# A hybrid attention block: 128-row products for the low part of k, operands at one place in 512 bytes, and a second half of w_out that enters early

## The chip, the cores and the metric

The kernel runs on one core of a Trainium2 chip. The metric is the device time of one execution in microseconds. Three runs of the kernel before gave a median of 910.77 us (908.93 to 912.34). TensorE is called PE, VectorE DVE, ScalarE ACT, GpSimd POOL, and SyncE SP; PEld is PE's loading of weights.

## The reference, cut to what matters

The block has 512 tokens of width 1024, 8 attention heads of 64, 8 retention heads with keys of 64 and values of 128, and an inner width of 4096. All data is fp32.

```python
ada = (c_act @ w_ada[l] + b_ada[l])[:, None, :]
sh1, sc1, g1, sh2, sc2, g2 = jnp.split(ada, N_ADA, axis=-1)
h = modulate(rms_norm(x, ln1_w[l]), sh1, sc1)
proj = h @ w_in[l]
mq, mk, mv, rq, rk, rv, rg, ga, gr = jnp.split(proj, split_at, axis=-1)
mq = apply_rotary(to_heads(mq, MOBA_HEADS), moba_cos, moba_sin)
mk = apply_rotary(to_heads(mk, MOBA_HEADS), moba_cos, moba_sin)
a_out = moba_attention(mq, mk, to_heads(mv, MOBA_HEADS))   # scores q.k, softmax, times v
y_a = from_heads(a_out) @ w_moba_o[l]
rq = apply_rotary(to_heads(rq, RET_HEADS), ret_cos, ret_sin)
rk = apply_rotary(to_heads(rk, RET_HEADS), ret_cos, ret_sin)
r_out = retention_chunkwise(rq, rk, to_heads(rv, RET_HEADS))  # scores q.k, decayed, times v
r_out = head_group_norm(r_out, ret_gn_w[l]).astype(x.dtype)
y_r = (jax.nn.silu(rg) * r_out) @ w_ret_o[l]
merged = jax.nn.sigmoid(ga) * y_a + jax.nn.sigmoid(gr) * y_r
x = x + g1 * (merged @ w_out[l])
h2 = modulate(rms_norm(x, ln2_w[l]), sh2, sc2)
x = x + g2 * (jnp.square(jax.nn.relu(h2 @ w_ff1[l])) @ w_ff2[l])
return rms_norm(x, final_norm_w)
```

## The kernel before

Every fp32 operand of a large product is split in two: a high part, and a low part that holds what the high part leaves. `mm3` (L214) then issues three matmuls, high by high, high by low and low by high, for one 128x512 piece (L215 to L217). A weight comes from HBM by a DMA of SP into one of three `raw` buffers; ACT writes its high part `whi` (L179) and POOL its low part `wlo` in four pieces (L184).

The stages follow each other in the span: the conditioning vector and the first norm (0 to 67 us); attention, with the projections of its heads, up to about 228; retention, with its projections, to 415; the gates to 441.7; the merge of both branches with the first half of w_out's columns, 441.7 to 513.8; w_out's second half with the second norm, to 548; the first product of the MLP (FF1) to 723, the second (FF2) to 897; the last norm.

**Scores.** Two heads are stacked in the 128 partitions. `kh` holds the high part of k for each of the two, with zeros in the other head's 64 partitions, so `q` of both heads meets it in a product of 128 rows (L547, L682). The low part `kl` holds both heads without zeros, and its product takes 64 rows of `kl` and of `q` (L548 and L683). The pieces of work that prepare the next pair of heads wait in a list `later` and are taken one by one between products. A head has four score products, of 128, 256, 384 and 512 columns, each followed by its product with `kl`, so there are 32 products of 64 rows in attention and 32 in retention.

**Merge.** `merge(i2)` (L955) makes 256 columns of y_r (48 matmuls with `zh`, `zl`), and for each of their two halves DVE multiplies by the gate (`sgr`, L958), adds the attention branch (`m`, L960), ACT writes `mh` (L961) and DVE `ml` (L962), the operands of w_out. Between these, `advance(background)` takes one step of `ada_steps`: the gate vector g1 is made by 16 steps of two DVE instructions each (L780, L782, L785), each on a DMA of 256 KB into one of two buffers `ada_raw`; after each four steps comes a split (`ada_hi` on ACT, `ada_lo` on DVE) and two small matmuls on PE (L756, L757). The loop at L968 then follows each of merge 1 to 3 with w_out's first half for the two k that are ready, 12 matmuls for each of eight k, into the four accumulators `wo0`; a scheduler sets the final order in this stage.

**w_out's second half and the second norm.** For each of four row blocks t, `out_product` gives 24 matmuls with `woh` and `wol`, which `load_late` made. After the residual, `square` (ACT) and `scale2` (DVE, L1034 and L1035) norm the block, `turn2` transposes it on PE (L1045) and brings it back by four instructions on DVE (L1052) and four on ACT (L1050), and `split2` writes FF1's operands `h2h` and `h2l` (L223, L224). In this part the order on PE, DVE and ACT is the order of the code.

A tile's address in SBUF follows from the sizes of the tiles that its pool has given out before it.

Of the kernel before, what the change touches and what calls it, by code (L numbers as in the profile page):

```python
# [8 lines left out]
F32 = mybir.dt.float32  # L9
# [18 lines left out]
def block_kernel(  # L28
# [116 lines left out]
    cols = G.tile([P, 72], F32, name="cols")  # L145
    cols1 = G.tile([P, 72], F32, name="cols1")

# [307 lines left out]

    later, stacked = deque(), []

    def do_later(n):
        for _ in range(min(n, len(later))):
            later.popleft()()  # L460

# [25 lines left out]
    def stack_q(i, t):  # L487
# [8 lines left out]
        qk[i] = [q]  # L496

    def stack_k(i, t):
        kh = A1.tile([P, 2, S], F32R, name="kh", tag="kh", bufs=2)
        kl = A1.tile([P, S], F32R, name="kl", tag="kl", bufs=2)  # L500

        def copies(s):
            own, other = halves(s)
            ACT.activation(kh[own, s, :], t[own, :], AF.Copy)
            ACT.activation(kh[other, s, :], t[own, :], AF.Copy)

        def rest(s):
            own, _ = halves(s)
            DVE.tensor_sub(kl[own, :], t[own, :], kh[own, s, :].bitcast(F32))

        later.extend((lambda: copies(0), lambda: rest(0), lambda: copies(1), lambda: rest(1)))
        later.append(lambda: stacked.append(i))
        qk[i] += [kh, kl]

# [22 lines left out]
    def moba_scores(h, t):  # L537

        while h // 2 not in stacked:
            do_later(1)  # L540
        q, kh, kl = qk[h // 2]
        s, pb = h % 2, 64 * (h % 2)
        own = slice(pb, pb + 64)
        n = (t + 1) * P
        ts = slice(t * P, n)
        sc = ps("S")
        PE.matmul(sc[:, :n], q[:, s, ts], kh[:, s, :n], start=True, stop=False)  # L547
        PE.matmul(sc[:, :n], q[own, s, ts], kl[own, :n], start=False, stop=True)  # L548
        pr = A1.tile([P, S], F32, name="pr", tag="pr", bufs=4)
        st = A1.tile([P, 8], F32, name="stat", tag="stat", bufs=6)  # L550
        DVE.tensor_tensor(sc[:, ts], sc[:, ts], cap, op=ALU.min)
# [81 lines left out]

    eh = A1.tile([P, 224], F32R, name="eh")
    es = A1.tile([P, 4], F32R, name="es")
# [35 lines left out]
    def ret_scores(h, kt):  # L671
        while 4 + h // 2 not in stacked:
            do_later(1)
        q, kh, kl = qk[4 + h // 2]
        s, pb = h % 2, 64 * (h % 2)
        own = slice(pb, pb + 64)
        if kt == 0 and h < 7:
# [4 lines left out]
        PE.matmul(sc[:, :n], kh[:, s, js], q[:, s, kt * P :], start=True, stop=False)  # L682
        PE.matmul(sc[:, :n], kl[own, js], q[own, s, kt * P :], start=False, stop=True)  # L683
        pr = A1.tile([P, S], F32, name="pr", tag="pr", bufs=4)
# [55 lines left out]


    mod2 = G.tile([P, 2, 8], F32, name="mod2")

# [211 lines left out]
    def merge(i2):  # L955
        for i, a in enumerate(proj_256(w_ret_o, i2 * 256, NK, zh, zl)):
# [5 lines left out]
            DVE.tensor_sub(ml[k], m32, mh[k].bitcast(F32))  # L962
            advance(background)
            advance(background)

    wo0 = [ps("S"), ps("S"), ps("PT"), ps("O")]
    background = ada_steps(A2, (2,), DVE, g1)
    next(background)  # L968
    merge(0)
    for i2 in range(4):  # L970
# [7 lines left out]
    drain(background)  # L978
    a2_stack.close()
# [24 lines left out]

    def load_late(k):

        raw = load_raw([(lambda t: t[:, 0:512], w_out[k * P : (k + 1) * P, 512:D])])
        hi = H.tile([P, 512], F32R, name=f"woh{k}", tag=f"hh{k}")
        lo = H.tile([P, 512], F32R, name=f"wol{k}", tag=f"hl{k}")
        with tc.issue_after(merged[4 + k // 2]):  # L1010
            split(raw[:, 0:512], hi, lo, ACT, POOL)
        return hi, lo

    for t in range(NT):
        residual(W2, t, 0, wo0[t], g1)
    wo_w = [load_late(k) for k in range(NK)]

    def out_product(t, a, ks):
        ts = slice(t * P, (t + 1) * P)
        for k in ks:  # L1020
            hi, lo = wo_w[k]
            mm3(a, mh[k][:, ts], ml[k][:, ts], hi, lo, k == 0, k == NK - 1)

# [73 lines left out]
    scale2(3)  # L1097
    split2(2, h32)
    first = [ps("acc") for _ in range(4)]
# [166 lines left out]
```

## Time and profile before

| | |
|---|---|
| median of three runs | 910.77 us (908.93 to 912.34) |
| time of the profiled execution | 911.24 us |
| its span | 909.2 us |
| PE busy | 878.2 us, 97% of the span |
| PEld busy | 708.5 us, 78% |
| DVE busy | 465.6 us, 51% |
| ACT busy | 409.1 us, 45% |
| POOL busy | 501.6 us, 55% |
| mean granted clock of PE | 0.994 |

The span runs from the first instruction to the last; the 2.04 us between it and the time of the same execution lie around it. The profiled execution is 0.47 us above the median. Matmuls overlap, so the time that one costs PE is read from start to start, not from its own length. In a row of the timeline the columns are the start in us, the length in us, the engine, the line, the operation, what it writes and what it reads with the shapes, and in brackets the idle time of the engine before it and what ended this. "64*128 64x512" means 64 rows of weights and 64 rows of moving data; a number after x counts instructions that one row stands for.

### The profile page before, as it was taken

Reading aid. Unit: us, or ns where it says so; the run is one execution under the profiler, and the core shown is the slowest. Engines: PE = TensorE matmul, PEld = TensorE weight load, DVE = VectorE, ACT = ScalarE, POOL = GpSimd, SP = SyncE. Lnnn points to the kernel's source line nnn. Section 1 sums busy time; section 2 is a strip of 40 time slices with the busy share of each in tenths; the row PEclk is TensorE's granted clock in tenths of the full one; section 3 lists DMA queues with packets and bytes.
Section 4 is the critical chain, followed back from the end, with each engine's and each line's share of the span. In section 5 each row is a group of like instructions: output and inputs, shape, how many; then the busy total and the mean of one; then the engine's idle time right before and its main releaser. Section 6 shows DMA issues by size and latency. Waiting matters only on the chain.

```text
span 909.2 us, 11772 instructions
## 1 busy us (share of the span) xinstructions
PE 878.2 (97%) x4138; PEld 708.5 (78%) x4138; DVE 465.6 (51%) x887; ACT 409.1 (45%) x697; POOL 501.6 (55%) x606
## 2 busy tenths in 40 slices
PE   7889999999999999999999889999999999999996
PEld 4667777789777888778888679888888888888885
DVE  5885676777776868883186776003304011122225
ACT  4446888986744636645232254222222211112124
POOL 3456343625543654564755475967777754444454
PEclk9899999999999999999999999999999999999999
DMA  9955222321353343422454733533432222222202
GB/s 273 277 152 166 66 77 64 94 70 47 117 160 120 118 149 115 151 71 70 139 172 152 251 109 95 158 98 114 138 102 94 95 93 93 96 95 97 100 30 93
DMA packets 104426, 108.41 MB, mean 119 GB/s; under 512 B 4832, under 2 KB 93232, under 8 KB 104368
## 3 DMA queue, kind: packets, MB, share of 16 engines
q1 hardware_dynamic: 104224, 107.41, 38.2%
q8 instruction: 32, 0.52, 0.2%
q14 instruction: 26, 0.21, 0.1%
q10 hardware_dynamic: 144, 0.26, 0.1%
HBM read 105.55 MB, written 2.10 MB: 118 GB/s over the span
## 4 chain that ended last, share of the span: by engine, by line
PE 79%; DVE 10%; DMA 5%; ACT 2%; POOL 2%; SPq 1%; issue 1%; POOLq 0%; DVEq 0%; ACTq 0%
PE ps_acc L215 21%; PE ps_acc L216 20%; PE ps_acc L217 20%; DMA ada_raw<-in_w_ada_dram 2%; DVE adaacc L267 2%; PE ps_S L217 2%; PE ps_S L216 2%; PE ps_S L215 2%; POOL wlo L184 1%; PE ps_S L683 1%; DVE adaacc L271 1%; PE ps_S L548 1%; DMA raw<-in_w_in_dram 1%; PE ps_PT L576 1%; PE ps_PT L216 1%
## 5 line engine op out<-in xcount | busy, mean ns | idle before, releaser
L184 POOL TENSOR_TENSOR wlo<-raw,whi 128x256 fp32r<-128x256 f32 x500 | 384.5, 800 | 272.6 <-ACT whi L179 265.0
L179 ACT ACTIVATE whi<-raw 128x1024 fp32r<-128x1024 f32 x126 | 132.5, 1056 | 196.5 <-PE ps_O L217 108.8
L215 PE MATMUL ps_acc<-hh,whi 128*128 128x512 f32 x304 | 125.4, 412 | 0.4 <-ACT sw L469 0.4
L217 PE MATMUL ps_acc<-hh,wlo 128*128 128x512 f32 x304 | 119.6, 393 | 0.0
L216 PE MATMUL ps_acc<-hl,whi 128*128 128x512 f32 x304 | 118.9, 391 | 0.0
L216 PE MATMUL ps_acc<-h2l,whi 128*128 128x512 f32 (+1 forms) x288 | 106.7, 371 | 0.9 <-POOL h2l L224 0.6
L215 PE MATMUL ps_acc<-h2h,whi 128*128 128x512 f32 (+1 forms) x288 | 106.6, 370 | 0.0
L217 PE MATMUL ps_acc<-h2h,wlo 128*128 128x512 f32 (+1 forms) x288 | 106.5, 370 | 0.0
L223 DVE CAST fh<-act 128x512 fp32r<-128x512 f32 x32 | 15.6, 495 | 137.7 <-PE ps_O L216 132.9
L215 PEld LDWEIGHTS ps_acc<-hh,whi 128*128 128x128 f32 x304 | 57.1, 188 | 17.0 <-issue 4.9
L217 PEld LDWEIGHTS ps_acc<-hh,wlo 128*128 128x128 f32 x304 | 57.1, 188 | 13.1
L216 PEld LDWEIGHTS ps_acc<-hl,whi 128*128 128x128 f32 x304 | 57.2, 188 | 9.9
L216 PEld LDWEIGHTS ps_acc<-h2l,whi 128*128 128x128 f32 x288 | 54.3, 189 | 11.2 <-POOL h2l L224 0.8
L217 PEld LDWEIGHTS ps_acc<-h2h,wlo 128*128 128x128 f32 x288 | 54.1, 188 | 10.1
L215 PEld LDWEIGHTS ps_acc<-h2h,whi 128*128 128x128 f32 x288 | 54.1, 188 | 9.9
L216 PE MATMUL ps_acc<-wlo,fh 128*128 128x512 f32 (+1 forms) x136 | 52.7, 387 | 0.0
L215 PE MATMUL ps_acc<-whi,fh 128*128 128x512 f32 (+1 forms) x136 | 52.7, 387 | 0.0
L217 PE MATMUL ps_acc<-whi,fl 128*128 128x512 f32 (+1 forms) x136 | 52.6, 387 | 0.0
L782 DVE SCALAR_TENSOR_TENSOR ada_acc<-ada_raw,cact,ada_acc 128x256 f32<-128x256 f32 x48 | 34.2, 712 | 34.7 <-DMA ada_raw<-in_w_ada_dram 33.8
L1117 ACT ACTIVATE relu<-ps_acc 128x512 f32<-128x512 f32 x32 | 18.9, 589 | 67.8 <-PE ps_acc L217 64.9
L758 DVE TENSOR_TENSOR g<-g,ps_acc 128x256 f32<-128x256 f32 x8 | 3.3, 418 | 89.7 <-PE ps_acc L757 89.7
L1118 POOL TENSOR_TENSOR act<-relu 128x512 f32<-128x512 f32 x32 | 34.6, 1082 | 20.0 <-ACT relu L1117 20.0
(283 smaller groups left out, 1898.4 us busy)
## 6 DMA issues: line engine op xcount, KB each, us to landing
raw<-in_w_ff_dram SPq DMA_DIRECT2D x64, 512.0 KB, 3.3
raw<-in_w_in_dram SPq DMA_DIRECT2D x32, 512.0 KB, 3.8
ada_raw<-in_w_ada_dram SPq DMA_DIRECT2D x64, 256.0 KB, 3.1
raw<-in_w_in_dram SPq DMA_DIRECT2D x36, 256.0 KB, 3.5
wada<-in_w_ada_dram SPq DMA_DIRECT2D x32, 256.0 KB, 5.2
x<-in_x_dram SPq DMA_DIRECT2D x8, 512.0 KB, 5.5
raw<-in_w_ret_o_dram SPq DMA_DIRECT2D x8, 512.0 KB, 3.6
dec<-in_k_decay_dram SPq DMA_DIRECT2D x8, 256.0 KB, 4.5
```

The costliest lines, as they stand in the source:

```text
L179: ACT.activation(hi, raw, AF.Copy)
L184: eng.tensor_sub(lo[:, qs], raw[:, qs], hi[:, qs].bitcast(F32))
L215: PE.matmul(o, lh, rh, start=first, stop=False)
L216: PE.matmul(o, lh, rl, start=False, stop=False)
L217: PE.matmul(o, ll, rh, start=False, stop=last)
L223: eh.tensor_copy(hi, src)
L267: DVE.scalar_tensor_tensor(a[k % 2], ada[j][:, k, :], cact[:, k : k + 1], a[k % 2], op0=ALU.mult, op1=ALU.add)
L271: DVE.tensor_add(a[0], a[0], a[1])
L548: PE.matmul(sc[:, :n], q[own, s, ts], kl[own, :n], start=False, stop=True)
L782: eng.scalar_tensor_tensor(acc, raw[:, 0, :], cact[:, 2 * k2 : 2 * k2 + 1], acc, op0=ALU.mult, op1=ALU.add)
L1117: ACT.activation(r, a, AF.Relu)
L1118: POOL.tensor_mul(act[n], r, r)
```

## The change

1. The low part of k gets two tiles `kls`, made once, one for each of the two stacked heads. POOL writes zeros into the other head's half once. The product with it takes all 128 rows. Since the two tiles are used for every pair of heads, the write of the next pair's low part stays in the list until the last score product of the same half of the pair before is issued (`scored`). The small tile `stat` of the softmax has 16 buffers instead of 6.
2. Two tiles are longer by an unused piece (`cols1` by 32 fp32, `eh` by 16), and `mod2` is allocated earlier. All operands of the matmuls then begin at byte 480 of a block of 512 bytes. Before, `whi`, `wlo`, `qs` and `kh` began at 288, `hh`, `hl`, `woh`, `wol`, `mh`, `ml`, `fh` and `fl` at 352, and `h2h`, `h2l`, `zh`, `zl`, `ah`, `al`, `th`, `tl` and `vm` at 480.
3. In the merge, three steps of g1's making come after each half instead of two, for merges 0 to 2, and none in merge 3; what is left is drained before the loop's last round. The first four `load_late` come in the third round of the loop, and 12 matmuls of w_out's second half (row block 0, k 0 to 3) into a new accumulator `wo1` come before the last 24 of its first half.
4. In the second norm the product of blocks 2 and 3 is cut at another place: four (t = 2) or two (t = 3) of the eight k come before the transposes of block t - 2. Block 2 is scaled after the split of block 1, and the split of block 2 comes before the scaling of block 3. `split2` gives its second low part to POOL only for t of 2 and 3, else to DVE.

```diff
-    cols1 = G.tile([P, 72], F32, name="cols1")
+    cols1 = G.tile([P, 72 + 32], F32, name="cols1")[:, :72]
+    mod2 = G.tile([P, 2, 8], F32, name="mod2")
...
     def do_later(n):
         for _ in range(min(n, len(later))):
-            later.popleft()()
+            if isinstance(later[0], tuple):
+                if later[0][0] not in scored:
+                    return
+                later.popleft()[1]()
+            else:
+                later.popleft()()
...
+    kls = [A1.tile([P, S], F32R, name=f"kl{s}") for s in range(2)]
+    for s in range(2):
+        POOL.memset(kls[s][halves(s)[1], :].bitcast(F32), 0.0)
...
-        kl = A1.tile([P, S], F32R, name="kl", tag="kl", bufs=2)
...
-            DVE.tensor_sub(kl[own, :], t[own, :], kh[own, s, :].bitcast(F32))
+            DVE.tensor_sub(kls[s][own, :], t[own, :], kh[own, s, :].bitcast(F32))
+
+        def rest_of(s):
+            return (2 * i - 2 + s, lambda: rest(s)) if i else lambda: rest(s)
...
-        PE.matmul(sc[:, :n], q[own, s, ts], kl[own, :n], start=False, stop=True)
+        PE.matmul(sc[:, :n], q[:, s, ts], kls[s][:, :n], start=False, stop=True)
+        if t == 0:
+            scored.add(h)
...
-    eh = A1.tile([P, 224], F32R, name="eh")
+    eh = A1.tile([P, 224 + 16], F32R, name="eh")[:, :224]
...
-        PE.matmul(sc[:, :n], kl[own, js], q[own, s, kt * P :], start=False, stop=True)
+        PE.matmul(sc[:, :n], kls[s][:, js], q[:, s, kt * P :], start=False, stop=True)
+        if kt == NT - 1:
+            scored.add(8 + h)
...
-            advance(background)
-            advance(background)
+            for _ in range(3 if i2 < 3 else 0):
+                advance(background)
...
     for i2 in range(4):
         if i2 < 3:
             merge(i2 + 1)
+        else:
+            drain(background)
+            wo1 = ps("acc")
+            out_product(0, wo1, range(4))
         hi, lo = load_512(w_out, 2 * i2, 0)
+        if i2 == 2:
+            wo_w = [load_late(k) for k in range(4)]
...
-            split(h32[jg], h2h[:, js, ts], h2l[:, js, ts], DVE, POOL if jg else DVE)
+            split(h32[jg], h2h[:, js, ts], h2l[:, js, ts], DVE, POOL if jg and t >= 2 else DVE)
...
     for t in range(NT):
-        a = ps("acc")
-        out_product(t, a, range(4))
+        a = ps("acc") if t else wo1
+        ks = range(4 if t == 0 else 0, NK)
         if t >= 2:
+            out_product(t, a, ks[: 8 - 2 * t])
             h32 = turn2(t - 2)
...
             split2(t - 2, h32)
-        out_product(t, a, range(4, NK))
+            if t == 3:
+                scale2(2)
+            ks = ks[8 - 2 * t :]
+        out_product(t, a, ks)
...
-        if t < 3:
+        if t < 2:
             scale2(t)
...
-    h32 = turn2(2)
+    split2(2, turn2(2))
     scale2(3)
-    split2(2, h32)
```

PE at the end of merge 0, before the change (a number behind a name is that of the tile; `zh_4604` belongs to the last of the eight heads):

```order
L215 MATMUL ps_acc<-zh_4604,whi 128x512
L216 MATMUL ps_acc<-zl_4605,whi 128x512
L217 MATMUL ps_acc<-zh_4604,wlo 128x512
L215 MATMUL ps_acc<-zh_4141,whi 128x512
L216 MATMUL ps_acc<-zl_4142,whi 128x512
L217 MATMUL ps_acc<-zh_4141,wlo 128x512
L215 MATMUL ps_acc<-zh_4181,whi 128x512
```

After the last three matmuls of merge 0 those of merge 1 follow, which need nothing new but weights. The same place of PE's order after the change:

```order
L218 MATMUL ps_acc<-zh_4600,whi 128x512
L219 MATMUL ps_acc<-zl_4601,whi 128x512
L220 MATMUL ps_acc<-zh_4600,wlo 128x512
L218 MATMUL ps_S<-whi,mh_4615 128x512
L219 MATMUL ps_S<-wlo,mh_4615 128x512
L220 MATMUL ps_S<-whi,ml_4623 128x512
L218 MATMUL ps_S<-whi,mh_4615 128x512
L219 MATMUL ps_S<-wlo,mh_4615 128x512
```

The first products of w_out (`mh_4615` and `ml_4623`, the operands of k = 0) now stand directly behind merge 0, ahead of merge 1; 14 of them stand there.

PE in the third round of the loop after the change, between merge 2 and merge 3 (`mh_4617` is k = 2):

```order
L773 MATMUL ps_acc<-ada_hi,ones 128x256
L774 MATMUL ps_acc<-ada_lo,ones 128x256
L218 MATMUL ps_S<-whi,mh_4617 128x512
L219 MATMUL ps_S<-wlo,mh_4617 128x512
L220 MATMUL ps_S<-whi,ml_4625 128x512
L218 MATMUL ps_S<-whi,mh_4617 128x512
L219 MATMUL ps_S<-wlo,mh_4617 128x512
L220 MATMUL ps_S<-whi,ml_4625 128x512
L773 MATMUL ps_acc<-ada_hi,ones 128x256
L218 MATMUL ps_PT<-whi,mh_4617 128x512
L219 MATMUL ps_PT<-wlo,mh_4617 128x512
L220 MATMUL ps_PT<-whi,ml_4625 128x512
```

The matmuls of g1's third group of steps and of its fourth stand here, with six products between them. Before the change the fourth pair stood behind all of w_out's first half.

DVE in merge 3, before the change (`ml_4633` and `ml_4634` are k = 6 and 7):

```order
L785 SCALAR_TENSOR_TENSOR ada_acc<-ada_raw,cact,ada_acc 128x256
L782 SCALAR_TENSOR_TENSOR ada_acc<-ada_raw,cact,ada_acc 128x256
L785 SCALAR_TENSOR_TENSOR ada_acc<-ada_raw,cact,ada_acc 128x256
L958 TENSOR_TENSOR sgr<-sgr,ps_acc 128x512
L960 TENSOR_TENSOR m_5086<-ma_4060,sgr 128x512
L962 TENSOR_TENSOR ml_4633<-m_5086,mh_4625 128x512
L958 TENSOR_TENSOR sgr<-sgr,ps_acc 128x512
L758 TENSOR_TENSOR g_4617<-g_4617,ps_acc 128x256
L960 TENSOR_TENSOR m_5104<-ma_4085,sgr 128x512
L224 TENSOR_TENSOR ada_lo<-ada_acc,ada_hi 128x256
L962 TENSOR_TENSOR ml_4634<-m_5104,mh_4626 128x512
```

Steps of g1 stand ahead of `sgr` and between the gates. DVE in merge 3, after the change (`ml_4629` and `ml_4630` are k = 6 and 7):

```order
L775 TENSOR_TENSOR g_4613<-g_4613,ps_acc 128x256
L975 TENSOR_TENSOR sgr<-sgr,ps_acc 128x512
L977 TENSOR_TENSOR m_5107<-ma_4056,sgr 128x512
L979 TENSOR_TENSOR ml_4629<-m_5107,mh_4621 128x512
L975 TENSOR_TENSOR sgr<-sgr,ps_acc 128x512
L977 TENSOR_TENSOR m_5112<-ma_4081,sgr 128x512
L979 TENSOR_TENSOR ml_4630<-m_5112,mh_4622 128x512
```

Only the last addition to g1 (`g_4613`) stands ahead; no step of g1 is left here.

DVE in the second norm, before the change, around the residual of block 2 (`x_2`):

```order
L223 CAST h2h<-h_32_5374 128x4x128
L1002 TENSOR_TENSOR u<-ps_acc,g_4617 128x512
L1003 TENSOR_TENSOR x_2_5196<-x_2_5196,u 128x512
L1034 RECIPROCAL rs_5422<-rs_5422 128x1
L1035 TENSOR_SCALAR y_5421<-x_2_5196,rs_5422 128x1024
L1052 TENSOR_SCALAR h_32_5449<-ps_S,mod_692 128x128 x4
L223 CAST h2h<-h_32_5449 128x4x128
L224 TENSOR_TENSOR h2l<-h_32_5449,h2h 128x4x128
L223 CAST h2h<-h_32_5450 128x4x128
```

The scaling of block 2 (`RECIPROCAL`, `y_5421`) comes directly behind its residual, and ahead of block 1's `h`. The same place after the change:

```order
L1042 TENSOR_TENSOR u<-ps_acc,g_4613 128x512
L1043 TENSOR_TENSOR x_2_5229<-x_2_5229,u 128x512
L1077 TENSOR_SCALAR h_32_5437<-ps_S,mod_144 128x128 x4
L226 CAST h2h<-h_32_5437 128x4x128
L227 TENSOR_TENSOR h2l<-h_32_5437,h2h 128x4x128
L226 CAST h2h<-h_32_5438 128x4x128
L227 TENSOR_TENSOR h2l<-h_32_5438,h2h 128x4x128
L1059 RECIPROCAL rs_5418<-rs_5418 128x1
L1060 TENSOR_SCALAR y_5417<-x_2_5229,rs_5418 128x1024
```

The four instructions of `h`, two casts and two subtractions of block 1 come first, and then the scaling of block 2.

## Rows read from the trace of the kernel before

**Rows 1.** Stretches: PE, PEld, DVE, ACT, POOL busy, clock, DMA share, GB/s

```profile
25.00:31.00 6.00, 6.00 (x18) 4.93 (x19) 5.36 (x9) 2.94 (x5) 3.38 (x2) 0.50 1.19 301
92.00:228.00 136.00, 135.22 (x707) 109.47 (x706) 94.79 (x278) 112.94 (x245) 59.81 (x75) 1.00 0.23 67
240.00:415.00 175.00, 174.88 (x866) 140.75 (x866) 130.90 (x225) 92.02 (x150) 86.94 (x101) 1.00 0.41 127
441.70:513.80 72.10, 69.05 (x298) 54.54 (x298) 46.19 (x64) 20.76 (x32) 44.97 (x48) 1.00 0.49 162
513.80:548.00 34.20, 31.48 (x178) 26.82 (x176) 26.54 (x47) 15.14 (x29) 16.91 (x19) 1.00 0.55 182
730.00:870.00 140.00, 140.00 (x601) 112.20 (x600) 28.37 (x50) 26.43 (x25) 71.42 (x102) 1.00 0.28 92
```

**Rows 2.** PE's timeline in attention: score products L547, L548 and what follows

```profile
122.01 0.47 PE L547 MATMUL ps_S<-kh,qs 128*128 128x512 f32 x1
...
122.84 0.50 PE L215 MATMUL ps_acc<-hh,whi 128*128 128x512 f32 x1
123.18 0.40 PE L216 MATMUL ps_acc<-hl,whi 128*128 128x512 f32 x1
...
183.74 0.36 PE L547 MATMUL ps_S<-kh,qs 128*128 128x256 f32 x1
...
184.34 0.33 PE L547 MATMUL ps_S<-kh,qs 128*128 128x128 f32 x1
...
184.85 0.51 PE L215 MATMUL ps_acc<-hh,whi 128*128 128x512 f32 x1
```

**Rows 3.** PE's timeline in retention: score products L682, L683 and their neighbours

```profile
239.75 0.33 PE L585 MATMUL ps_O<-tl,vm 128*128 128x128 f32 x1
239.92 0.44 PE L682 MATMUL ps_S<-qs,kh 128*128 128x512 f32 x1
...
240.71 0.50 PE L215 MATMUL ps_acc<-hh,whi 128*128 128x512 f32 x1
...
256.23 0.22 PE L682 MATMUL ps_S<-qs,kh 128*128 128x128 f32 x1
...
256.63 0.50 PE L215 MATMUL ps_acc<-ah,whi 128*128 128x512 f32 x1
```

**Rows 4.** PEld's timeline in attention: weight loads

```profile
122.41 0.18 PEld L548 LDWEIGHTS ps_S<-kl,qs 64*128 64x128 f32 x1 [0.24 <-issue]
...
122.95 0.19 PEld L216 LDWEIGHTS ps_acc<-hl,whi 128*128 128x128 f32 x1
```

**Rows 5.** PE's timeline: w_out's second half, 39 matmuls apart, FF1, 33 apart

```profile
514.50 0.39 PE L215 MATMUL ps_acc<-woh,mh 128*128 128x512 f32 x1
...
523.34 0.39 PE L215 MATMUL ps_acc<-woh,mh 128*128 128x512 f32 x1
...
566.00 0.40 PE L216 MATMUL ps_acc<-h2l,whi 128*128 128x512 f32 x1
...
573.70 0.39 PE L216 MATMUL ps_acc<-h2l,whi 128*128 128x512 f32 x1
```

**Rows 6.** DVE's timeline in the merge: first and eighth step of g1

```profile
453.25 0.35 DVE L780 TENSOR_SCALAR ada_acc<-ada_raw,cact 128x256 f32<-128x256 f32 x1 [10.55 <-DMA ada_raw<-in_w_ada_dram]
...
470.91 0.49 DVE L785 SCALAR_TENSOR_TENSOR ada_acc<-ada_raw,cact,ada_acc 128x256 f32<-128x256 f32 x1
```

**Rows 7.** ACT's timeline in merges 0 and 1

```profile
456.53 0.63 ACT L961 ACTIVATE mh<-m 128x512 fp32r<-128x512 f32 x1 [8.02 <-DVE m L960]
457.06 1.04 ACT L179 ACTIVATE whi<-raw 128x1024 fp32r<-128x1024 f32 x1
...
462.28 0.42 ACT L221 ACTIVATE ada_hi<-ada_acc 128x256 fp32r<-128x256 f32 x1 [1.12 <-DVE ada_acc L785]
```

**Rows 8.** PE's timeline: first matmul of merge 1

```profile
452.95 0.39 PE L215 MATMUL ps_acc<-zh,whi 128*128 128x512 f32 x1
```

**Rows 9.** PE's timeline in the second norm: transposes of block 1

```profile
539.38 0.33 PE L1045 MATMUL ps_S<-ident,y 128*128 128x128 f32 x1 [1.83 <-ACT h L1050]
```

More of the change, by code (lines that the diff above doesn't have):

```diff
@@ L453, in project_pair @@
         )
-    later, stacked = deque(), []
+    later, stacked, scored = deque(), [], set()
     def do_later(n):
         for _ in range(min(n, len(later))):
-            later.popleft()()
+            if isinstance(later[0], tuple):
[4 more added lines that the diff above has]
+                later.popleft()()
     def rope(i, part, a, stack):
@@ L508, in rest @@
             own, _ = halves(s)
-            DVE.tensor_sub(kl[own, :], t[own, :], kh[own, s, :].bitcast(F32))
-        later.extend((lambda: copies(0), lambda: rest(0), lambda: copies(1), lambda: rest(1)))
+            DVE.tensor_sub(kls[s][own, :], t[own, :], kh[own, s, :].bitcast(F32))
+        def rest_of(s):
+            return (2 * i - 2 + s, lambda: rest(s)) if i else lambda: rest(s)
+        later.extend((lambda: copies(0), rest_of(0), lambda: copies(1), rest_of(1)))
         later.append(lambda: stacked.append(i))
-        qk[i] += [kh, kl]
+        qk[i] += [kh]
     vm = []
@@ L540, in moba_scores @@
             do_later(1)
-        q, kh, kl = qk[h // 2]
-        s, pb = h % 2, 64 * (h % 2)
-        own = slice(pb, pb + 64)
+        q, kh = qk[h // 2]
+        s = h % 2
         n = (t + 1) * P
@@ L547, in moba_scores @@
         PE.matmul(sc[:, :n], q[:, s, ts], kh[:, s, :n], start=True, stop=False)
-        PE.matmul(sc[:, :n], q[own, s, ts], kl[own, :n], start=False, stop=True)
+        PE.matmul(sc[:, :n], q[:, s, ts], kls[s][:, :n], start=False, stop=True)
+        if t == 0:
+            scored.add(h)
         pr = A1.tile([P, S], F32, name="pr", tag="pr", bufs=4)
-        st = A1.tile([P, 8], F32, name="stat", tag="stat", bufs=6)
+        st = A1.tile([P, 8], F32, name="stat", tag="stat", bufs=16)
         DVE.tensor_tensor(sc[:, ts], sc[:, ts], cap, op=ALU.min)
@@ L673, in ret_scores @@
             do_later(1)
-        q, kh, kl = qk[4 + h // 2]
-        s, pb = h % 2, 64 * (h % 2)
-        own = slice(pb, pb + 64)
+        q, kh = qk[4 + h // 2]
+        s = h % 2
         if kt == 0 and h < 7:
@@ L737, in ret_norm @@
         split(zf, zh[h], zl[h], ACT, POOL)
-    mod2 = G.tile([P, 2, 8], F32, name="mod2")
     def ada_steps(work, which, eng, dst=None):
@@ L969, in block_kernel, with load_late, out_product @@
     merge(0)
+    def load_late(k):
+        raw = load_raw([(lambda t: t[:, 0:512], w_out[k * P : (k + 1) * P, 512:D])])
+        hi = H.tile([P, 512], F32R, name=f"woh{k}", tag=f"hh{k}")
+        lo = H.tile([P, 512], F32R, name=f"wol{k}", tag=f"hl{k}")
+        with tc.issue_after(merged[4 + k // 2]):
+            split(raw[:, 0:512], hi, lo, ACT, POOL)
+        return hi, lo
+    def out_product(t, a, ks):
+        ts = slice(t * P, (t + 1) * P)
+        for k in ks:
+            hi, lo = wo_w[k]
+            mm3(a, mh[k][:, ts], ml[k][:, ts], hi, lo, k == 0, k == NK - 1)
     for i2 in range(4):
@@ L977, in block_kernel @@
                 mm3(wo0[t], mh[k][:, ts], ml[k][:, ts], hi[:, k % 2, :], lo[:, k % 2, :], k == 0, k == NK - 1)
-    drain(background)
     a2_stack.close()
@@ L1003, in residual @@
         DVE.tensor_add(x2[t][:, hs], x2[t][:, hs], u)
[L1005 to L1012, printed above, removed]
     for t in range(NT):
         residual(W2, t, 0, wo0[t], g1)
[L1016 to L1022, printed above, removed]
+    wo_w += [load_late(k) for k in range(4, NK)]
     ys = {}
```

## The prediction, made before the changed kernel ran

> **What bounds the kernel now.** I read the table of busy shares first: PE is busy 97% of the span, so time is gained only by work that PE does in less time or by stalls of PE that go. Then I cut the span into the stages of the program [rows 1]. PE has no idle time to speak of in attention (135.22 of 136.00 us) and retention (174.88 of 175.00), none in FF2 (140.00 of 140.00); it lacks 3.05 of 72.10 us in the merge and 2.72 of 34.20 in the stretch of the second norm. The helpers stand close behind PE in two places: ACT has 112.94 of 136 us in attention (83%), DVE 130.90 of 175 in retention (75%). Third, PE's timeline where the score products stand [rows 2, 3]; fourth, its pace in long runs of equal matmuls [rows 5]; and last, DVE, ACT and PE at the entry to the merge [rows 6 to 8].
>
> **Term 1, the 64-row products become 128-row ones.** The cost of a pair is read from its first start to the start of what follows. In attention the pair of 512 columns takes 122.84 - 122.01 = 0.83 us, that of 256 takes 0.60, that of 128 takes 0.51 [rows 2]; 0.71 for 384 columns is between its neighbours (estimate). A head pays 2.65 us. The 128-row matmul behind the 512 pair takes 0.34 [rows 2], where such matmuls follow each other at 0.23 [rows 5]; three of a head's four pairs are followed by one, so 0.33 more. In retention the 512 pair takes 0.79 and the 128 pair 0.40 [rows 3], the two between some 0.64 and 0.52 (estimate): 2.35 for a head, and four times 0.11 behind. Why the mixed pairs cost so much is seen on PEld: the weights of the matmul that starts at 123.18 are loaded from 122.95, under the 128-row matmul that runs since 122.84 [rows 2, 4]; those of the 64-row product are loaded only at 122.41, after 0.24 us without a load [rows 4].
>
> Without 64-row products I price a score matmul as its columns at the pace of the long runs: 0.233, 0.175, 0.117, and 0.09 for 128 columns (0.058 by columns alone, and 0.17 at most, which is what the 128-column product before the scores takes [rows 3]). A head then pays 2 x 0.615 = 1.23. Attention saves 8 x (2.65 - 1.23 + 0.33) = 14.0, retention 8 x (2.35 - 1.23 + 0.44) = 12.5.
>
> Not all of it reaches the end. With 14 us less of PE, ACT's 112.9 us would fill 93% of what is left of that stretch, and DVE's 130.9 81% of retention's. I take 9 of attention's 14.0, since ACT would be the busiest helper anywhere in the kernel there, and all of retention's: **-21.5**. Bounds: -26.5 when nothing else becomes late; -9 when ACT holds attention at its present length and DVE a quarter of retention's gain. The write of the next pair's low part now waits for the last scores of the pair before; queued behind it on DVE are the softmax and the splits of the current head, with ACT and then PE's transposes waiting for those. It stays in the list until those scores are issued, so DVE isn't parked on it for long, and I price it at nothing within these bounds; the same for the two memsets on POOL, which is busy 59.81 of 136 us.
>
> The Trainium skill speaks against this term: "TensorE: Matmul & The Clock Gate" (The mechanism) says that a weight load overlaps running matmuls only when its row group differs, so products of all 128 rows would load their weights in the open. By it the sum of this term would be 0, and that is rival F. The load at 122.95, under a running product of 128 rows, disagrees [rows 4].
>
> **Term 2, all operands at one place in 512 bytes.** The pace differs today between operands. FF1 (`h2h` at 480, `whi` at 288) runs at 7.70 / 33 = 0.2333 us, w_out's second half (both operands at 352) at 8.84 / 39 = 0.2267 [rows 5], and FF2 (`fh` 352, `whi` 288) at 140 / 601 = 0.2329 [rows 1]. If equal places are what makes w_out's pace, FF1's 672 matmuls of 512 columns save 672 x 0.0066 = 4.4 us and FF2's 768 save 768 x 0.0062 = 4.8; the projections' `hh` products (352 against 288) I put at 1.8 by the same difference on some 270 of them, since part of their gain is in term 1's stretches, where helpers hold. **-11.0**. Bounds: 0 (the pace of w_out has another cause, such as the state of the stage around it) and -14 (all projections gain in full).
>
> **Term 3, the merge, w_out and the second norm.** DVE's first ten instructions of the merge stand in the same order as before. So the first step of g1 still waits for its DMA until 453.25, 10.55 us of idle [rows 6], `mh` of k = 0 still ends at 456.53 + 0.63 = 457.16, and the first `ada_hi` at 462.28 + 0.42 = 462.70 [rows 7]. PE ends merge 0 at 452.95 [rows 8]. Before, merge 1 stood there and covered all this; now 14 products of w_out and that `ada_hi` do. Fourteen products last 14 x 0.233 = 3.3 us, so PE would be through at 456.2 and gets on at 462.7: a **stall of 6.5 us**. Then merge 1 follows, and DVE's `sgr` of merge 1 comes later by as much.
>
> The second stall is at the fourth group of g1's steps, which PE meets six products behind merge 2. Without it PE would be there 14 + 48 + 10 + 48 + 6 = 126 products and six small matmuls behind 452.95: 126 x 0.2267 + 0.7 = 29.3, plus 6.5, at 488.7. The first eight steps took 471.40 - 453.25 = 18.15 us [rows 6], 2.27 each, and at that pace the sixteenth ends at 489.6, its `ada_hi` at 490.0. DVE and ACT have the merge's own work in between, `sgr` and `m` (0.7 each on DVE, an estimate from `mh` of the same shape), `mh` 0.63 and a `whi` 1.04 [rows 7], 3.0 together: 493.0. **Stall 4.3.** In turn, the 3.05 us of idle time that this stage has today goes, as no step of g1 is left for merge 3. Its 288 matmuls save 288 x 0.0066 = 1.9 by term 2's reason. So 6.5 + 4.3 - 3.05 - 1.9 = **+5.8**.
>
> The second norm I put at nothing. Today's wait of 1.83 us at the transposes of block 1 [rows 9] goes, since more of the product stands ahead of them; but block 2 is now scaled behind block 1's `h`, casts and subtractions, so the transposes of block 2 come due when DVE has four more instructions ahead of `y`, and two further subtractions per block go from POOL to DVE, which has 26.54 of 34.20 us there [rows 1]. Bounds of this part: -3 (all idle time of the stretch) to +4. Bounds of term 3: -7 (3.05 + 1.9 + 1.8 gained, no stall) to +13 (+5.8 with 4 in the norm, and 3.05 when today's idle time doesn't go).
>
> **The sum.** 911.2 (the profiled execution's own time) - 21.5 - 11.0 + 5.8 = **884.5 us**. That execution is 0.5 above the median of the runs, well within what the runs differ by, so I leave it.
>
> **The rivals.** (B) The scheduler's early steps of g1 come in time, and the merge has no stall: term 3 is -6.8. For it: DVE is busy only 46.19 of 72.10 us there [rows 1], so it has time to run g1's steps ahead of PE. Against it: the DMA that ends at 453.25. 911.2 - 21.5 - 11.0 - 6.8 = 871.9. (C) The place of the operands does nothing: term 2 is 0 and the 1.9 of the merge stays, 911.2 - 21.5 + 7.7 = 897.4. For it: only one kind of product shows the faster pace; against it: that product differs from FF2's in little else. (D) ACT becomes the bound of attention: term 1 is -9, 897.0. For it: the 83%; against it: ACT also works ahead into other heads. (F) A 128-row product's weights aren't loaded ahead when both products of a pair are of 128 rows, term 1 is 0: 906.0, just at the edge of what can be told from no change (0.5%, 4.6 us). Against it: 174.88 of 175.00 busy at 0.23 a matmul. (E) It gets slower: the stalls in the merge make PE's granted clock fall from 2.4 to 1.2 GHz. In the stretch from 25 to 31 us the granted clock is 0.50 with PE busy throughout [rows 1]; at that level each us of PE's work costs a second one. 26 us of such work bring the forecast back to today's time, and it decides from 31, where the time is slower by more than can be told from no change: 884.5 + 31 = 915.5. Against it: PE's idle times of 1.83 and 3.05 us today were followed by a clock of 1.00 [rows 1, 9].
>
> **How the numbers follow.** Forecast 0.50, B 0.20, C 0.12, D 0.08, F 0.05, E 0.05. The range from 868 to 902 holds A, B, C and D, with the bounds of their costs at the ends; F, E and what is beyond B's bound are left out. The forecast's own range is 876 to 893. Faster by over 0.5%: A to D and most of F's half, 0.92; within 0.5%: the rest of F, 0.04; slower: most of E, 0.04.
>
> **What would show it.** Term 1: score pairs at 0.47 for 512 columns, and their following matmul at 0.23; ACT's share of attention over 90% with waits of PE for ACT would show D. Term 2: FF1 and FF2 at 0.227 from start to start; 0.233 would show C. Term 3: PE idle behind merge 0 for an `mh`, an `ml` and an `ada_hi`, 6.5 us together, and again behind merge 2, by some 4 us. The prediction is wrong if the span of attention and retention shrinks by less than 12 us, or if the merge stage gets shorter.

## The result and the profile after

The changed kernel takes 905.96 us (median of 5 runs, 903.67 to 906.67) where the kernel before takes 910.77: a ratio of 0.9942 with the interval [0.9922, 0.9962]. It is faster, by about 5 us; 884.5 was forecast, with a range that ended at 902. The span of the profiled execution is 904.6 us, against 909.2.

Both traces have the same 4138 matmuls, so the same instruction can be looked up in both. Up to the first scores of attention the changed kernel gains 1.4 us, in attention and retention together 10.2, from the merge to the end of the first 256-column part of FF1 it **loses 16.1**, and in the rest of FF1 and FF2 it gains 9.0.

From the page of the kernel after, PE's line of part 1 and the granted clock of part 2:

```profile
PE 856.2 (95%) x4138; PEld 713.6 (79%) x4138; DVE 465.0 (51%) x889; ACT 409.2 (45%) x697; POOL 501.8 (55%) x606
PEclk9999999999999999999898998999999999999999
```

PE has 22 us less to do, and 17 us of that stand in the span as idle time (48.4 us instead of 31.0); the three 8s of the clock are the slices that begin at 430, 475 and 543 us, in merge and norm. What PE waits for in the kernel after:

```profile
PE ps_acc L773 <- ACT ada_hi L224: 6.6, 1, 6.6
PE ps_S L1070 <- DVE y L1060: 5.2, 1, 5.2
PE ps_S L218 <- ACT mh L978: 4.6, 1, 4.6
PE ps_O L602 <- ACT th L224: 2.1, 4, 0.7
PE ps_O L603 <- DVE tl L227: 1.4, 4, 0.4
```

The first three are new at this length, and all three lie in merge and norm; `th` and `tl` are the high and low part of the transposed scores, the operands of the product with v. Stretches of the kernel after, columns as in [rows 1]; the first two lie in attention and retention, the next three hold the three waits, the last is in FF2:

```profile
90.00:224.00 134.00, 130.85 (x720) 110.41 (x719) 94.92 (x280) 114.06 (x248) 60.79 (x76) 1.00 0.23 69
235.00:404.00 169.00, 165.39 (x868) 140.99 (x869) 133.40 (x226) 92.33 (x151) 89.74 (x102) 1.00 0.42 131
441.00:456.00 15.00, 9.99 (x32) 7.46 (x32) 10.72 (x19) 2.63 (x4) 3.88 (x4) 0.77 0.52 166
478.00:490.00 12.00, 5.38 (x16) 4.09 (x15) 7.77 (x13) 4.18 (x7) 5.80 (x6) 0.72 0.20 68
532.00:546.00 14.00, 8.78 (x44) 7.63 (x43) 12.28 (x23) 5.87 (x14) 6.71 (x8) 0.82 0.44 132
720.00:860.00 140.00, 140.00 (x619) 115.95 (x618) 27.59 (x50) 28.11 (x27) 74.32 (x105) 1.00 0.28 96
```

Attention and retention now have over 3 us of idle PE each, where [rows 1] had 0.8 and 0.1; FF2 runs 619 matmuls in 140 us where it ran 601, 0.2262 us each. And PE's timeline in the kernel after, at the places of [rows 2], [rows 3], [rows 5] and [rows 8], and at the second and third wait:

```profile
119.83 0.48 PE L563 MATMUL ps_S<-kh,qs 128*128 128x512 f32 x1
120.14 0.39 PE L564 MATMUL ps_S<-kl,qs 128*128 128x512 f32 x1
120.37 0.40 PE L218 MATMUL ps_acc<-hh,whi 128*128 128x512 f32 x1
120.61 0.40 PE L219 MATMUL ps_acc<-hl,whi 128*128 128x512 f32 x1
...
234.82 0.33 PE L602 MATMUL ps_O<-th,vm 128*128 128x128 f32 x1 [0.74 <-ACT th L224]
235.31 0.44 PE L699 MATMUL ps_S<-qs,kh 128*128 128x512 f32 x1
...
235.82 0.40 PE L218 MATMUL ps_acc<-hh,whi 128*128 128x512 f32 x1
...
440.81 0.39 PE L220 MATMUL ps_acc<-zh,wlo 128*128 128x512 f32 x1
445.81 0.79 PE L218 MATMUL ps_S<-whi,mh 128*128 128x512 f32 x1 [4.62 <-ACT mh L978]
...
448.01 0.63 PE L218 MATMUL ps_S<-whi,mh 128*128 128x512 f32 x1
448.44 0.63 PE L219 MATMUL ps_S<-wlo,mh 128*128 128x512 f32 x1
448.87 0.63 PE L220 MATMUL ps_S<-whi,ml 128*128 128x512 f32 x1
...
485.43 0.58 PE L773 MATMUL ps_acc<-ada_hi,ones 128*128 128x256 f32 x1 [6.62 <-ACT ada_hi L224]
...
542.57 1.97 PE L1070 MATMUL ps_S<-ident,y 128*128 128x128 f32 x8 [5.22 <-DVE y L1060]
...
569.96 0.40 PE L219 MATMUL ps_acc<-h2l,whi 128*128 128x512 f32 x1
...
577.46 0.39 PE L219 MATMUL ps_acc<-h2l,whi 128*128 128x512 f32 x1
```

The pair of 512 columns takes 120.37 - 119.83 = 0.54 us in attention (0.83 before) and 0.51 in retention (0.79), and the matmul behind it 0.24 (0.34). FF1's two rows are 33 matmuls apart: 0.2273 each (0.2333). And behind the wait for `mh` a matmul takes 0.43 us, where 0.227 is the pace: TensorE is at the lower of its levels, 1.2 GHz. The same happens once in attention, at its start, where PE waits 1.52 us for `kh` and 0.34 for `kl`:

```profile
87.70 0.63 PE L220 MATMUL ps_acc<-hh,wlo 128*128 128x512 f32 x1
88.12 0.63 PE L218 MATMUL ps_acc<-hh,whi 128*128 128x512 f32 x1
```

Nine matmuls from 86.89 us on cost some 1.6 us more by this. The kernel before has the same two waits there (1.50 and 0.32 us) and goes on at 0.23. On PEld the load for the product with `kl` is now ahead of it (119.91, under the product from 119.83):

```profile
119.91 0.19 PEld L564 LDWEIGHTS ps_S<-kl,qs 128*128 128x128 f32 x1
```

DVE and ACT in the kernel after, as [rows 6] and [rows 7]; the last DVE row is the scaling of block 2, the last ACT row the fourth `ada_hi`:

```profile
441.86 0.35 DVE L797 TENSOR_SCALAR ada_acc<-ada_raw,cact 128x256 f32<-128x256 f32 x1 [10.76 <-DMA ada_raw<-in_w_ada_dram]
...
481.86 0.48 DVE L802 SCALAR_TENSOR_TENSOR ada_acc<-ada_raw,cact,ada_acc 128x256 f32<-128x256 f32 x1
...
541.49 1.02 DVE L1060 TENSOR_SCALAR y<-x,rs 128x1024 f32<-128x1024 f32 x1
```

```profile
445.13 0.63 ACT L978 ACTIVATE mh<-m 128x512 fp32r<-128x512 f32 x1 [8.37 <-DVE m L977]
...
484.97 0.40 ACT L224 ACTIVATE ada_hi<-ada_acc 128x256 fp32r<-128x256 f32 x1
```

The DMA in front of g1's first step comes about as long after the retention as before (10.76 us of idle DVE against 10.55), and the sixteenth step ends at 482.34, 40.5 us later; on ACT an `mh`, a `woh` and a `whi` come before its `ada_hi`.

### The profile page after: what moved, and what is told of

Read it like the earlier page. It is cut to its first block, busy times and chain, and to the rows that moved or that the text cites. A ratio compares the mean times of both kernels' runs of the same rounds, so it can differ in the third digit from the quotient of the medians.

```text
span 904.6 us, 11771 instructions
## 1 busy us (share of the span) xinstructions
PE 856.2 (95%) x4138; PEld 713.6 (79%) x4138; DVE 465.0 (51%) x889; ACT 409.2 (45%) x697; POOL 501.8 (55%) x606
## 4 chain that ended last, share of the span: by engine, by line
PE 67%; DVE 16%; DMA 7%; ACT 7%; issue 3%; SPq 0%; POOL 0%; ACTq 0%; DVEq 0%
PE ps_acc L218 17%; PE ps_acc L219 17%; PE ps_acc L220 17%; DMA ada_raw<-in_w_ada_dram 4%; DVE adaacc L270 2%; PE ps_S L219 2%; PE ps_S L218 2%; PE ps_S L220 2%; DMA wada<-in_w_ada_dram 2%; DVE ada_acc L802 1%; DVE ada_acc L799 1%; DVE adaacc L274 1%; PE ps_PT L220 1%; PE ps_PT L219 1%; PE ps_PT L218 1%
## 5 line engine op out<-in xcount | busy, mean ns | idle before, releaser
L218 PE MATMUL ps_acc<-hh,whi 128*128 128x512 f32 x304 | 121.5, 400 | 0.0
L218 PEld LDWEIGHTS ps_acc<-h2h,whi 128*128 128x128 f32 x288 | 55.1, 191 | 8.6
L219 PEld LDWEIGHTS ps_acc<-h2l,whi 128*128 128x128 f32 x288 | 55.1, 191 | 8.5
L799 DVE SCALAR_TENSOR_TENSOR ada_acc<-ada_raw,cact,ada_acc 128x256 f32<-128x256 f32 x48 | 31.2, 650 | 35.9 <-DMA ada_raw<-in_w_ada_dram 35.2
```

The lines of the kernel that those rows point to most:

```text
L218: PE.matmul(o, lh, rh, start=first, stop=False)
L219: PE.matmul(o, lh, rl, start=False, stop=False)
L799: eng.scalar_tensor_tensor(acc, raw[:, 0, :], cact[:, 2 * k2 : 2 * k2 + 1], acc, op0=ALU.mult, op1=ALU.add)
```

## The experiments

The first four take the change apart. All their ratios are to the kernel before, with 95% intervals.

**The 128-row products alone.** The edits on `kls`, `scored` and `stat`, nothing else. (A tile's place follows from the tiles before it, so `th` and `tl`, at byte 480 in both kernels, lie at 288 in this run and at 160 in the next.)

> The kernel before with the 128-row products of the low part of k alone (with their gate in the list and the 16 stat buffers); operands stay at their old places, merge and norm as before. Theory 1 (helpers hold part of the gain): score products and their followers get cheaper by about 20 us in all, but PE then waits for ACT's th and DVE's tl in attention and retention, and the time falls by only 9 to 11 us, to about 901. Rival (the price of the products was wrong, PE itself is slower than priced and does not wait): also about 901, but with no new waits of PE at the lines of th and tl. Forecast on record (term 1): 889.

899.12 us, ratio 0.9872 [0.9857, 0.9886]. Summed over all matmuls of attention and retention from start to start, the score products and their followers got 23.2 us cheaper, and 12.4 came back, most of it in front of products that read `th` and `tl`. Theory 1 stands: the price of the products was near the forecast, the waits were not.

**The places alone.** `cols1`, `eh` and `mod2`.

> The kernel before with the two paddings and the earlier mod2 alone. Theory: every long run of 512-column products goes from 0.233 to 0.227 us: FF1 4.4, FF2 4.8 to 5.1, the merge 1.9, projections 1 to 3, so 12 to 14 us faster, 897 to 899. Rival (the faster pace in the changed kernel comes from its other edits): no change, 911.

899.79 us, 0.9875 [0.9859, 0.9892]. In its trace FF1 and FF2 gain 9.0 us; attention and retention gain nothing (360.7 us against 358.8 for the same matmuls; some 1.6 of the difference is a stretch at 1.2 GHz from 86.7 us on, as in the kernel after). So the pace of the two long products comes with the place of their operands, and the 1.8 us that I had added for the projections do not. Whether it is the equal place of both operands or byte 480 itself, no run tells apart; w_out's second half had the pace before, with both at 352.

**Both together.**

> Both of these together, merge and norm as before. Theory (all of the loss of the changed kernel lies in the order of merge and norm): stages up to 441 us gain 11.9, FF1 and FF2 9.0, merge and norm about 2.5 by the pace: 887 to 889, and the granted clock stays at 1.00 from the gates to FF1. Rival (the clock falls in merge and norm because PE has become faster, whatever the order): 892 to 896, with slices of a lower clock after 440 us.

890.08 us, 0.9768 [0.9754, 0.9783]: between theory and rival by the time. No slice of the clock in merge and norm falls below 9 tenths, but it does not stay at 1.00 either: the stretch from 427 to 500 us has 0.98 and that from 500 to 538 has 0.96, with matmuls at 0.43 us behind a wait of 3.50 us for `mh`. So the rival holds in part: with merge and norm as before, the lower clock costs some 3 us in this trace (half of PE's time at 1.2 GHz, an estimate), and nothing in the kernel before. Without its merge and norm the change is worth 21 us; with them 5.

**The new norm on top.** Old merge.

> The same with the new order of the second norm added (cut of the product, block 2 scaled later, second low part of blocks 0 and 1 on DVE), merge as before. Theory (the norm's order makes its own wait): PE waits about 5 us for y of block 2 and then runs some 12 us of work at a lower clock, 2.5 us lost; less the 2.7 us of idle time that the old order has: 5 us slower than the run without it, 892 to 894. Rival (the wait for y comes from what the merge leaves behind, w_out's residuals late on DVE): no difference, 888.

893.51 us, 0.9808 [0.9790, 0.9826], 3.4 more than without it. Its trace has the wait of the kernel after:

```profile
PE ps_S L1062 <- DVE y L1052: 5.2, 1, 5.2
```

So the merge has the other 12 us (905.96 less 893.51, ratios 0.9942 and 0.9808). The next three look for the part of the merge that does it.

**PE pinned to the code's order in the new merge**, with the old norm.

```diff
+    pinned = tc.manual_schedule(engines={mybir.EngineType.PE})
+    pinned.__enter__()
     background = ada_steps(A2, (2,), DVE, g1)
...
+    pinned.__exit__(None, None, None)
```

> 128-row products, places and the new merge (three steps of g1 after a half, the early second half of w_out), the old norm, and PE's order in the merge pinned to that of the code: merge 0, merge 1, then k 0 and 1, merge 2, and so on. Theory (the loss of 12.4 us between this change's merge and the old one comes from PE's order, in which w_out's first products and the fourth pair for g1 stand too early): the waits for mh, ada_hi and the lower clock behind them go, 888 to 891. Rival (g1's steps are late whatever PE's order, because three steps after a half need their DMAs sooner): waits for ada_hi of some 5 us stay, 896 to 903.

905.15 us, 0.9938 [0.9917, 0.9959]. My theory fell: with w_out's first products behind merge 1 the wait for `mh` is gone, and the time isn't back. In this order PE waits for the first `ada_hi` instead, right behind merge 0, and 3.69 us for the fourth:

```profile
451.19 0.58 PE L773 MATMUL ps_acc<-ada_hi,ones 128*128 128x256 f32 x1 [10.09 <-ACT ada_hi L224]
...
452.06 0.63 PE L218 MATMUL ps_acc<-zh,whi 128*128 128x512 f32 x1
452.49 0.63 PE L219 MATMUL ps_acc<-zl,whi 128*128 128x512 f32 x1
```

**Two steps of g1, but the early second half of w_out; and three steps, without it.** Both with the old norm and the scheduler's own order; the edit shown is that of the first, against the changed kernel.

```diff
-            for _ in range(3 if i2 < 3 else 0):
+            for _ in range(2):
```

> 128-row products, places, old norm, and of the merge's change only the early second half of w_out (its first four load_late and 12 products ahead of the last 24 of the first half): two steps of g1 after each half in all four merges, as before. Theory (the third step alone puts the pairs for g1 on PE ahead of their DMAs, and w_out's early second half costs nothing): no wait for ada_hi over 2 us, clock 1.00 in merge and norm, 887 to 891. Rival (the early loads of w_out compete with g1's DMAs and with the merge on ACT): 895 to 903.

890.47 us, 0.9766 [0.9737, 0.9795].

> 128-row products, places, old norm, and of the merge's change only the three steps of g1 after each half of merges 0 to 2 (none in merge 3); w_out's second half as before. Theory: the loss of 12 us comes with it, waits of PE for mh and ada_hi of 4 to 7 us each with the clock at 1.2 GHz behind them, 900 to 904. Rival (as in the run beside it): 888 to 892.

901.49 us, 0.9899 [0.9875, 0.9923]. Against the run with the old merge (0.9768) the first differs by w_out's early second half alone, the second by the order of g1's steps alone (three after a half, none in merge 3). This pair settles it: the third step costs 11 us, w_out's early second half nothing. PE's waits in the merge, first with two steps, then with three:

```profile
PE ps_acc L774 <- DVE ada_lo L227: 2.1, 1, 2.1
...
PE ps_acc L773 <- ACT ada_hi L224: 1.9, 1, 1.9
```

```profile
PE ps_acc L773 <- ACT ada_hi L224: 6.9, 1, 6.9
PE ps_S L218 <- ACT mh L978: 4.7, 1, 4.7
```

The clock was not 1.00 throughout with two steps either: behind its two waits some eight matmuls ran at 0.43 us.

**PE kept busy through the wait.** The pinned run, with 44 matmuls whose result is thrown away in front of the first `ada_hi`.

```diff
+                if i == 2 and n0 == 0:
+                    for _ in range(44):
+                        PE.matmul(cp, zh[0][:, 0:P], zl[0], start=True, stop=True)
                 PE.matmul(cp[:, 0:256], ones, hi, start=True, stop=False)
```

> The run with the pinned merge, with 44 extra matmuls of 512 columns, whose result is thrown away, in the place where PE stood for 10.1 us in front of the first ada_hi. Theory (a wait of that length costs more than itself, since the 13 matmuls behind it run at 0.427 in place of 0.227 us, at a granted clock of 1.2 GHz): PE reaches the same point at the same time, these 13 run at 0.227 and the time falls by 2.6 us, to 902 to 903. Rival (the slow pace behind the wait comes from something else, the loads of w_out and of g1 arriving at that moment): pace and time stay, 905.

905.05 us, 0.9943 [0.9923, 0.9963], no gain. But the pace behind the wait did change, from 0.43 to 0.23 us:

```profile
449.34 0.40 PE L218 MATMUL ps_acc<-zh,whi 128*128 128x512 f32 x1
449.57 0.40 PE L219 MATMUL ps_acc<-zl,whi 128*128 128x512 f32 x1
```

Merge 1 is then 2.1 us earlier, and PE waits 6.25 us for the fourth `ada_hi` instead of 3.69 in that run, so the 2.1 us are lost there. That `ada_hi` starts 54.7 us after the first matmul of the merge in the pinned run, 55.1 here, 54.8 in the changed kernel and 54.2 with the three steps alone: g1's chain, from its DMAs by DVE's steps to ACT's split, sets the end of the stretch in all four, though their orders on PE differ. Which link holds it (the two buffers for the DMAs, DVE or ACT) wasn't tried. So the slow matmuls are the price of the wait, as the theory had it (8 of them, not 13), but that price reaches the end only where no later wait takes it up. What I expected of the time was wrong.

**Block 2 scaled early**, in the new norm.

```diff
             out_product(t, a, ks[: 8 - 2 * t])
+            if t == 3:
+                scale2(2)
             h32 = turn2(t - 2)
```

> 128-row products, places, old merge, new norm, but block 2 is scaled ahead of the transposes of block 1, as in the kernel before, and not behind block 1's split. Theory (the wait of 5.2 us for y of block 2 comes from its place on DVE behind block 1's h, casts and subtractions): that wait goes, at most 2 us of it come again elsewhere, 888 to 890. Rival (DVE has too much in this stretch, with the second low part of blocks 0 and 1 on it): some wait of PE for DVE stays, 892 to 895.

892.76 us, 0.9796 [0.9773, 0.9820], against 0.9808 [0.9790, 0.9826] with the late scaling: the intervals overlap. The wait for block 2's `y` went, and two others came:

```profile
PE ps_S L1062 <- ACT h L1067: 2.5, 1, 2.5
...
PE ps_S L1062 <- DVE y L1052: 1.3, 1, 1.3
```

The place on DVE made that one wait, but the time didn't follow it. What else in the new norm costs the 3 us (the low parts that went from POOL to DVE are left) stays open; no run undid them alone.

The last four ask why attention and retention gave only half.

**No gate.** Gate means here the condition `scored`, by which the write of the next low part waits. The low part of k stays in one tile for two heads, and the product takes all its rows; `q` holds the low part of q in the other head's rows, so what is added is a product of two low parts.

```diff
-        PE.matmul(sc[:, :n], q[own, s, ts], kl[own, :n], start=False, stop=True)
+        PE.matmul(sc[:, :n], q[:, s, ts], kl[:, :n], start=False, stop=True)
...
```

> 128-row products and places, old merge and norm, but the low part of k stays one tile of two heads in two buffers as in the kernel before, so its write waits for nothing and POOL writes no zeros (but once, for the first pair). The 128-row product then adds to each score the product of the low part of q with the other head's low part of k, two low parts, of the size that the kernel leaves out anyway. Theory (PE waits for ACT and DVE because the products in front of the values have become shorter): the waits at th and tl in attention and retention stay, about 10 us in all, 889 to 891. Rival (the gate shifts DVE's and ACT's work to a worse place): most of these waits go, 880 to 884.

893.34 us, 0.9809 [0.9790, 0.9828], slower than with the gate. Its waits at `th` and `tl` are as many: 14.9 us before products that read a split, against 12.4 with the gate. The gate isn't the cause; why the run is 3 us slower wasn't sought.

**One piece of projection moved** from a head's first transposes to its last values, with the gate; and **both edits**.

```diff
-            if kt == 0:
-                fill(1)
             th, tl, _ = moba_turn(h, kt)
...
-            fill(1)
+            fill(2 if kt == 3 else 1)
             do_later(1)
```

> 128-row products and places, old merge and norm, with the gate, and one of nine pieces of projection work of each attention head moved: from in front of the head's transposes to in front of its last values, where no scores stand. Theory (th and tl are late where the least work stands between transposes and values): the waits before the last values of a head (128 columns, 0.2 to 0.8 us and 0.2 to 0.5 at each) go, some new ones come at the first, 886 to 889. Rival (ACT is busy all the time and only its total counts): no change, 890; or slower by up to 4 where the first transposes now wait for the softmax.

888.05 us, 0.9754 [0.9731, 0.9777]. The waits for `th` in attention went and three for `attn`, the sum behind a head's values, of up to 0.8 us came. In its trace attention is 2.6 us shorter and retention 1.6 longer, 1.0 together, less than the times can tell apart.

> Both of the last two edits together, with the same added product of low parts. Theory: the sum of their two effects, 885 to 889. Rival (gate is the cause): 878 to 883.

892.71 us, 0.9804 [0.9786, 0.9823]: as without the gate.

**Less work for ACT.** The softmax's last step, the division by the sum, is left out.

```diff
-        ACT.activation(pr[:, :n], pr[:, :n], AF.Copy, scale=st[:, 7:8])
```

> 128-row products and places, old merge and norm, and the softmax's last step on ACT (32 multiplications of the probabilities by the reciprocal of their sum, 0.4 to 0.7 us each) left out. Theory (PE waits in attention since ACT and the chain behind the scores are late now that the products cover less): the waits at th and tl of attention go, and attention gets 4 to 5 us shorter, 885 to 886. Rival (PE's products themselves take the time, ACT is not late): the waits and the time stay, 889 to 891.

884.97 us, 0.9725 [0.9704, 0.9746], against 0.9768 [0.9754, 0.9783]. Attention is 4.5 us shorter; ACT is busy 99.59 of 129 us there, and PE is idle for 1.7 us instead of 3.1:

```profile
90.00:219.00 129.00, 127.28 (x715) 109.54 (x714) 95.77 (x281) 99.59 (x216) 60.58 (x76) 1.00 0.24 71
```

So ACT and the chain behind the scores hold 4.5 us of attention; the edit takes away both work of ACT and a link of that chain, and which of the two counts it doesn't tell. Retention was left as it is by this run (-7.6 us, as with the division), and what holds it there, DVE or ACT, wasn't tried.

**The parts that gain or cost nothing, together** (128-row products, places, moved piece, two steps, early second half, old norm).

> The parts that gained or cost nothing together: 128-row products, places, one piece of projection work moved to a head's last values, two steps of g1 after each half, the early second half of w_out, the old norm. Theory: 887 to 889, and better than both kernels; rival (the two small edits get in each other's way): 890 to 892.

889.63 us, 0.9764 [0.9743, 0.9784]. Four kernels lie between 888 and 890.5 and can't be told apart; each beats both the kernel before and the changed one.

## Why the prediction was wrong

The direction was right, the size was not: 884.5 lies 21.5 us below the median and 22.2 below the profiled execution (906.67 us), from which the terms are read. Of the 22.2, 11.3 lie in term 1, 2.0 in term 2 and 10.3 in term 3, while 1.4 us were gained at the start where nothing was forecast. That the time came out at rival F's 906.0 is chance: its cause, loads that aren't ahead, is refuted by the load at 119.91 us.

**Term 1: -10.2 where -21.5 stood.** Under 12 us, as the prediction's own sign of being wrong had it. The gross price was close: 23.3 us went from the score products and their followers (26.5 forecast); a pair of 512 columns still takes 0.54 and not 0.47 in attention. The step that failed is "I take 9 of attention's 14.0 ... and all of retention's". Attention kept 3.2 and retention 7.0: the time before products that wait for a split rose from 0.8 to 6.6 us in attention and from 1.5 to 6.5 in retention (from start to start, over the pace of the long runs; the idle time of the stretches shows less, since matmuls overlap and a short pause between two starts leaves none). Another 1.6 us of attention's gain went to the nine matmuls at 1.2 GHz at its start. I had rival D's mechanism and its size (-9), looked at busy shares (83% and 75%) and took the smaller one for harmless; D's sign came by half, PE waits for ACT, but ACT's share is 85% (114.06 of 134.00 us) and not over 90%. A share says how much work a helper has in a stretch; PE waits for one chain from the scores by `th` and `tl` to the values, and that chain had been hidden by the 0.8 us pairs which became shorter. For attention the run without the division bears this out; for retention it is argued from the waits.

**Term 2: -9.0 where -11.0 stood.** FF1 and FF2 gained what was worked out. The 1.8 us for the projections were an addition without a row.

**Term 3: +16.1 where +5.8 stood.** The two stalls were found. Their sum is near (10.8 forecast, 11.6 measured), in part by luck: the first is 5.0 us (4.62 for `mh`, 0.40 for `ml`) where 6.5 stood, since the products behind it ran at 0.43 us and filled the time until `ada_hi`; the second is 6.62 where 4.3 stood, since the fourth `ada_hi` started 43.1 us after g1's first step and not 39.4. The steps that failed are two. First, "The second norm I put at nothing": block 2's `y` costs 5.22 us of waiting, where 1.83 went. It stands behind eight instructions of DVE that last 4.0 us together (I wrote four), and behind DVE's own wait for ACT's part of `h`, which I had not seen:

```profile
539.83 0.43 DVE L226 CAST h2h<-h 128x512 fp32r<-128x512 f32 x1 [1.41 <-ACT h L1075]
```

And of the subtractions one per block went from POOL to DVE, not two. Second, the clock, which I put at nothing outside rival E. Against E stood waits of 1.83 and 3.05 us followed by a clock of 1.00; but the 3.05 are the sum of two waits, so the rows held none of the length that I forecast:

```profile
505.56 0.50 PE L215 MATMUL ps_S<-whi,mh 128*128 128x512 f32 x1 [1.35 <-ACT mh L961]
511.11 0.50 PE L217 MATMUL ps_S<-whi,ml 128*128 128x512 f32 x1 [1.71 <-DVE ml L962]
```

From the merge to the end of FF1's first part PE's idle time rose by 11.1 us (5.8 to 16.9), matmuls at the lower clock, behind all three waits, cost 7.7 more (half of PE's time there, an estimate from the rows at 0.43 and 0.227), and the pace of all others gave some 2.7 back: 16.1. The pinned run lost the same with another order of PE, at other pairs of g1, and the run with two steps lost nothing: so the loss comes with the third step of g1 per half. In the kernel before, PE reached the fourth pair at 513.55 us, 71.8 after the merge's start, and its `ada_hi` started at 64.7; in the kernel after PE is there at 48.5 and `ada_hi` starts at 54.8.

In the description of the kernel before, one thing is wrong and bears on nothing above: `kh` holds a head's high part in both halves, and `qs` the high part of q in its own half and the low part in the other, so the first score product is high by high and low by high.

## What to carry to other kernels

When PE's products in front of a wait get cheaper, price the chain that they covered from its own rows (last input to first reader), not by its engine's busy share. A background job that is fed by DMAs should be met by PE no earlier than its chain ends; taking its steps sooner in the code moved its products up by 23 us in PE's queue, but the operand they read only by 10. And a forecast stall needs a price for the clock behind it, also where the same wait went without one before.

## What the runs showed of the hardware

- Behind waits of 4.62, 6.62 and 10.09 us matmuls of 512 columns took 0.43 us in place of 0.227, for about 8 to 14 of them, and behind the wait of 5.22 us 128- and 256-column ones 0.21; with PE kept busy through the longest the pace stayed at 0.23.
- For shorter waits the length alone doesn't tell. Behind 2.08 us (the places alone) eight matmuls ran at 0.43 us; behind 2.42 us (no gate, piece moved) the pace stayed. What decides between these two isn't shown.

```profile
504.98 0.50 PE L218 MATMUL ps_S<-whi,mh 128*128 128x512 f32 x1 [2.08 <-ACT mh L962]
...
507.30 0.63 PE L219 MATMUL ps_PT<-wlo,mh 128*128 128x512 f32 x1
507.73 0.63 PE L220 MATMUL ps_PT<-whi,ml 128*128 128x512 f32 x1
```

```profile
495.62 0.50 PE L218 MATMUL ps_S<-whi,mh 128*128 128x512 f32 x1 [2.42 <-ACT mh L962]
...
497.40 0.40 PE L218 MATMUL ps_PT<-whi,mh 128*128 128x512 f32 x1
497.63 0.39 PE L219 MATMUL ps_PT<-wlo,mh 128*128 128x512 f32 x1
```

- The place of the operands in 512 bytes moved the pace of the long products (0.2333 to 0.2273 in FF1, 0.2329 to 0.2262 in FF2), but not that of the projections, which ran at nearly the old sum; FF1's 256-column products went the other way, 0.1178 to 0.1200.
- A 128-row product, one half of which multiplies zeros, costs less than a 64-row one between 128-row products: 0.54 us for the pair of 512 columns, against 0.83.
